# Halving sums of weight blocks in pieces of 1024 columns: a decoder trunk on one Trainium2 core

## The chip, the cores and the metric

One core of a Trainium2 chip runs the whole program in one launch. The metric is device time in microseconds. PE is TensorE, DVE is VectorE, ACT is ScalarE, POOL is GpSimd, SP issues the loads.

## The reference

A decoder trunk of two layers over x of 512 tokens x 1024 features, in fp32. Each layer adds half a SwiGLU, then a mixer, then another half SwiGLU; a norm ends the trunk. So there are four SwiGLUs (called ffn 0 to 3 here), with the even mixer between ffn 0 and 1 and the odd one between ffn 2 and 3, and nothing between ffn 1 and 2:

```python
for l in range(DEPTH):                      # DEPTH = 2
    h = _rmsnorm(x, ffn_pre_norm[l])
    x = x + 0.5 * _swiglu(h, ffn_pre_w_gate[l], ffn_pre_w_up[l], ffn_pre_w_down[l])
    h = _rmsnorm(x, mix_norm[l])
    if l % 2 == 0:
        x = x + _retention_dilated_mixer(h, ab_w_in[l // 2], ab_w_out[l // 2])
    else:
        x = x + _gla_mixer(h, gla_w_in[l // 2], gla_w_a2[l // 2], gla_b_a[l // 2], gla_w_out[l // 2])
    h = _rmsnorm(x, ffn_post_norm[l])
    x = x + 0.5 * _swiglu(h, ffn_post_w_gate[l], ffn_post_w_up[l], ffn_post_w_down[l])

def _swiglu(h, wg, wu, wd):                 # hidden width 2816
    return (jax.nn.silu(h @ wg) * (h @ wu)) @ wd
```

## The kernel before, in words

Every fp32 matrix is split in two halves, a high one (a copy in the format fp32r, on ACT) and a low one (the rest, a subtraction on DVE), and every product is three matmuls: high x high, high x low, low x high (`mm3`, L205 to L207). x stays in SBUF as eight tiles of 128 features x 512 tokens.

An ffn has 22 tiles of 128 hidden features. The first four (HEAD = 2 pairs) are projected tile by tile (`proj_t`), while `moving` (L370) builds from x and the norm's row r the activations for the rest: for each of four k a tile hh (high, L387 and L392 on ACT) and hl (low, L393 and L394 on DVE), each with seven slots of 256 columns. The row r comes from sums of squares (POOL, L270), matmuls over ones (L280) and two diagonals (DVE, L296) that PE spreads over the partitions (L298); both diagonals use one buffer.

The other 18 tiles go in nine pairs, one `block` for gate and one for up, 18 blocks in an ffn and 72 in all. A block multiplies a 2 x 2 arrangement of weight quarters (A11, A12, A21, A22, 512 columns each) with a 2 x 2 arrangement of activations by the scheme of Strassen and Winograd: seven products (P0 to P6 here, in the order in which `block` calls `product`) of 12 matmuls of 256 columns in place of eight. It needs sums of weights, S1 to S4: S1 = A21 + A22, S2 = S1 less A11, S3 = A11 less A21, S4 = A12 less S2 (signs are put into the stored weights, so that each is an add). After two of its products a block calls `fill`, which runs a down-projection tile of an earlier group (12 matmuls of 512 columns in most groups). `save` copies partial results out of the accumulator (L414, ACT) before the next product overwrites it.

The weights come by a plan, a list of steps that `weights` works off ahead of their use as far as `room` lets it (three pieces ahead for whole tiles, AHEAD = 4 for sums). A block's steps are the nested functions of `block_plan` (L117): `c0` loads 1 MB as raw (L139, issued by SP; two buffers), halves the first two quarters as one piece of 1024 columns (L142, L147) and begins the sums; `s1`, `s2`, `s3`, `a22`, `s4` each halve one piece of 512 columns: `high` is the copy (L125, tile shi), `low` the subtraction (L131, tile slo), `add` the sums (L135). shi and slo have six buffers of 512 columns each (SUMS = 6). `run` puts a chunk of down weights (L106, L107: tiles whi, wlo) into the plan after four steps of a block.

The program is written in this order, and a scheduler then sets the order of each engine from it; an engine takes its instructions strictly in that order. A tile's buffer is reused when its last reader is done.

```python
return [("w", c0), ("s", s1), ("s", s2), ("s", s3), ("s", a22), ("s", s4)]
```

## Time and profile before

| what | value |
|---|---|
| time, median of 3 runs (range) | 1923.32 us (1918.73 to 1923.42) |
| the profiled execution, its own time | 1920.47 us |
| its span | 1918.7 us |
| PE busy | 1889.4 us |
| DVE busy | 1383.0 us |
| ACT busy | 850.2 us |
| POOL busy | 90.1 us |

The span runs from the first to the last instruction that the profiler saw; the execution's own time has 1.8 us around it. Times in a timeline are us from the start of the span. Matmuls overlap, so their pace is read from the starts of neighbours, not from the duration of one; DVE and ACT pieces overlap a little too.

In the timeline ffn 0 has its blocks from about 68 to 365 us, ffn 1 from 700 to 972, ffn 2 from 1042 to 1339 and ffn 3 from 1605 to 1897. The even mixer lies between 365 and 650, the odd one between 1339 and 1560. The heads of the four ffns are the stretches just ahead of their blocks; ffn 2 starts at about 995, when ffn 1's last down tiles end.

### The profile page before, as it was taken

What the parts mean: (1) busy time and instruction counts of PE and PEld (TensorE: products, weight loads), DVE (VectorE), ACT (ScalarE), POOL (GpSimd) and SP (SyncE); (2) the same over time, 40 slices, a digit from 0 to 9 for tenths busy, and PEclk for the clock granted to TensorE, in tenths of its full rate; (3) what the DMA queues carried; (4) which work ended last, traced back from release to release, by engine and by line L of the source; (5) the groups of instructions that cost most, each with busy time, mean ns of one, the idle gap of its engine ahead of it and who ended that gap; (6) DMA issues with size and microseconds to landing.
All of it is one profiled execution on the core that took longest, in us unless ns stands there. A gap on an engine that the chain in (4) does not pass through costs nothing.

```text
span 1918.7 us, 28135 instructions
## 1 busy us (share of the span) xinstructions
PE 1889.4 (98%) x11360; PEld 1660.4 (87%) x11360; DVE 1383.0 (72%) x2114; ACT 850.2 (44%) x1377; POOL 90.1 (5%) x69
## 2 busy tenths in 40 slices
PE   8999999999999999999999999999999999999996
PEld 6899999877777889999988999998788888999995
DVE  7987786744555897777679878776466579777864
ACT  5544444433332554444445444444434245544441
POOL 1000000200000200000020000002000020000001
PEclk9999999999999999999999999999999999999998
DMA  5222222321111423332132322222222142323211
GB/s 199 99 104 106 100 100 78 123 77 66 50 66 39 165 88 112 109 104 105 67 124 92 110 103 100 99 89 85 88 77 67 56 156 89 118 100 110 100 67 44
DMA packets 43061, 183.81 MB, mean 96 GB/s; under 512 B 4897, under 2 KB 7201, under 8 KB 33714
## 3 DMA queue, kind: packets, MB, share of 16 engines
q1 hardware_dynamic: 39888, 177.75, 26.6%
q10 hardware_dynamic: 3042, 4.26, 0.7%
q8 instruction: 89, 1.46, 0.3%
q14 instruction: 42, 0.34, 0.1%
HBM read 179.89 MB, written 2.10 MB: 95 GB/s over the span
## 4 chain that ended last, share of the span: by engine, by line
PE 95%; DVE 3%; issue 1%; ACT 0%; POOL 0%; DMA 0%; POOLq 0%; DVEq 0%; SPq 0%; ACTq 0%
PE pj L205 17%; PE pj L206 17%; PE pj L207 17%; PE pj L404 12%; PE pj L406 12%; PE pj L405 12%; PE sc L740 1%; PE o L768 1%; PE sc L280 1%; PE sc L298 0%; PE sc L815 0%; PE tp L756 0%; DVE xgl L253 0%; DVE wlo L107 0%; PE o L972 0%
## 5 line engine op out<-in xcount | busy, mean ns | idle before, releaser
L205 PE MATMUL pj<-xgh,whi 128*128 128x512 f32 x1260 | 506.2, 402 | 8.0 <-ACT whi L106 7.1
L206 PE MATMUL pj<-xgl,whi 128*128 128x512 f32 x1260 | 493.2, 391 | 1.1 <-DVE xgl L253 1.0
L207 PE MATMUL pj<-xgh,wlo 128*128 128x512 f32 x1260 | 492.6, 391 | 0.0
L405 PE MATMUL pj<-hl,shi 128*128 128x256 f32 x1440 | 404.9, 281 | 1.5 <-DVE hl L394 1.5
L404 PE MATMUL pj<-hh,shi 128*128 128x256 f32 x1440 | 405.0, 281 | 0.8 <-ACT hh L392 0.8
L406 PE MATMUL pj<-hh,slo 128*128 128x256 f32 x1440 | 404.7, 281 | 0.0
L106 ACT CAST whi<-wraw 128x1024 fp32r<-128x1024 f32 x189 | 197.8, 1047 | 254.2 <-PE pj L206 164.1
L125 ACT CAST shi<-raw 128x512 fp32r<-128x512 f32 x288 | 178.5, 620 | 288.1 <-PE pj L405 232.6
L205 PEld LDWEIGHTS pj<-xgh,whi 128*128 128x128 f32 x1260 | 238.2, 189 | 62.0 <-issue 12.1
L107 DVE TENSOR_TENSOR wlo<-wraw,whi 128x1024 fp32r<-128x1024 f32 x189 | 236.1, 1250 | 65.5 <-ACT whi L106 64.9
L207 PEld LDWEIGHTS pj<-xgh,wlo 128*128 128x128 f32 x1260 | 237.9, 189 | 50.3 <-DVE wlo L107 0.8
L406 PEld LDWEIGHTS pj<-hh,slo 128*128 128x128 f32 x1440 | 276.6, 192 | 0.1
L206 PEld LDWEIGHTS pj<-xgl,whi 128*128 128x128 f32 x1260 | 238.2, 189 | 43.2 <-DVE xgl L253 2.2
L405 PEld LDWEIGHTS pj<-hl,shi 128*128 128x128 f32 x1440 | 270.5, 188 | 4.6 <-DVE hl L394 1.7
L404 PEld LDWEIGHTS pj<-hh,shi 128*128 128x128 f32 x1440 | 270.5, 188 | 4.0 <-ACT hh L392 1.1
L131 DVE TENSOR_TENSOR slo<-raw,shi 128x512 fp32r<-128x512 f32 x288 | 197.1, 687 | 83.4 <-ACT shi L125 83.3
L405 PE MATMUL pj<-hl,whi 128*128 128x256 f32 x576 | 162.3, 282 | 0.5 <-DVE hl L393 0.5
L404 PE MATMUL pj<-hh,whi 128*128 128x256 f32 x576 | 162.3, 282 | 0.1
L406 PE MATMUL pj<-hh,wlo 128*128 128x256 f32 x576 | 162.0, 281 | 0.0
L135 DVE TENSOR_TENSOR raw<-raw 128x512 f32<-128x512 f32 x216 | 148.5, 688 | 3.0
L519 DVE SCALAR_TENSOR_TENSOR x<-pj,x 128x512 f32<-128x512 f32 x160 | 109.6, 685 | 50.7 <-PE pj L207 50.7
L270 POOL TENSOR_TENSOR sqa<-sqa,sq 128x512 f32<-128x512 f32 x41 | 64.0, 1561 | 1061.8 <-issue 645.2
(201 smaller groups left out, 2375.0 us busy)
## 6 DMA issues: line engine op xcount, KB each, us to landing
raw<-in_w_blk SPq DMA_DIRECT2D x72, 1024.0 KB, 4.8
wraw<-in_w_down SPq DMA_DIRECT2D x88, 512.0 KB, 3.2
wraw<-in_w_gu SPq DMA_DIRECT2D x32, 512.0 KB, 3.2
wraw<-in_w_dqk SPq DMA_DIRECT2D x8, 512.0 KB, 3.4
wraw<-in_w_rqk SPq DMA_DIRECT2D x8, 512.0 KB, 3.3
...
```

What stands on the lines that cost most here:

```text
L106: self.halved = nc.scalar.copy(out=hi[:, :cols], in_=raw[:, :cols]).ins
L107: nc.vector.tensor_tensor(out=lo[:, :cols], in0=raw[:, :cols], in1=hi[:, :cols].bitcast(F32), op=ALU.subtract)
L125: nc.scalar.copy(out=hi, in_=x)
L131: nc.vector.tensor_tensor(out=lo, in0=x, in1=hi.bitcast(F32), op=ALU.subtract)
L135: nc.vector.tensor_tensor(out=out, in0=a, in1=b, op=ALU.add)
L205: mm(out, lhsT=w[0], rhs=x[0], start=first, stop=False)
L206: mm(out, lhsT=w[0], rhs=x[1], start=False, stop=False)
L207: self.last = mm(out, lhsT=w[1], rhs=x[0], start=False, stop=last).ins
L404: mm(out, lhsT=w[0][:, s], rhs=hi, start=first and k == 0, stop=False, skip_group_check=True)
L405: mm(out, lhsT=w[0][:, s], rhs=lo, start=False, stop=False, skip_group_check=True)
L406: self.last = mm(out, lhsT=w[1][:, s], rhs=hi, start=False, stop=k == KD // 2 - 1, skip_group_check=True).ins
L519: nc.vector.scalar_tensor_tensor(out=self.x[d], in0=ps, scalar=0.5, in1=self.x[d], op0=ALU.mult, op1=ALU.add)
```

## The change

The quarters of a block are stored in the order A21, A22, A11, A12 instead of A11, A12, A21, A22 (the rows of numbers are the same, `blocks` on the host only swaps halves). So:

- S1 and S3 are neighbours: one add of 1024 columns, with A21 read twice by a broadcast, writes both into a tile s13 (one buffer).
- S2 is written over A21, so that S2 and A22 are neighbours in raw and are halved as one piece. S4 is written over A12.
- s13 and s2 are halved in pieces of 1024 columns in wide buffers, two for high and two for low halves. S4 stays a piece of 512 columns (thi, tlo, two buffers). c0 halves A11 and A12, the second half of raw, as before in 1024 columns.
- A block so has two wide halvings and one narrow in place of five narrow ones, and one wide add and two narrow in place of four narrow ones. `block` keeps s13 for its products P1 and P4, and s2 for P2 and P5.
- `room` lets fewer than two wide sums and fewer than two narrow ones be ahead, and the chunk of down weights comes after three steps of the plan.

```diff
--- before.py
+++ after.py
@@ -27,7 +27,7 @@
 EPS = 1e-6
 WC = 1024
 LOOK = 3
-AHEAD, SUMS = 4, 6
+SPACE = 16
 HELD = 4
 PASS3 = 0.65
 H = T // 2
@@ -91,7 +91,7 @@
 
     def room(self, kind):
         n = sum(k == kind for k, _ in self.ready)
-        return n <= LOOK if kind == "w" else n < AHEAD and len(self.ready) < AHEAD + 2
+        return n <= LOOK if kind == "w" else n < 2
 
     def load_w(self, src, cols):
         nc = self.nc
@@ -117,17 +117,16 @@
         st = {}
         q = [slice(i * T, (i + 1) * T) for i in range(4)]
 
-        def high(key, x):
+        def wide(x):
             if not self.spaced:
                 self.spaced = True
-                self.t2k(self.fpool, "space", bufs=1, shape=[P, 16])
-            hi = self.t2k(self.fpool, "shi", F32R, SUMS, shape=[P, T])
+                self.t2k(self.fpool, "space", bufs=1, shape=[P, SPACE])
+            hi = self.t2k(self.fpool, "shi", F32R, 2, shape=[P, WC])
+            lo = self.t2k(self.fpool, "slo", F32R, 2, shape=[P, WC])
             nc.scalar.copy(out=hi, in_=x)
-            st[key] = (hi, x)
-
-        def low(key):
-            hi, x = st[key]
-            lo = self.t2k(self.fpool, "slo", F32R, SUMS, shape=[P, T])
+            return hi, lo, x
+
+        def low(hi, lo, x):
             nc.vector.tensor_tensor(out=lo, in0=x, in1=hi.bitcast(F32), op=ALU.subtract)
             return hi, lo
 
@@ -139,37 +138,31 @@
             nc.sync.dma_start(out=raw, in_=src)
             hi = self.t2k(self.wpool, "whi", F32R, shape=[P, WC])
             lo = self.t2k(self.wpool, "wlo", F32R, shape=[P, WC])
-            nc.scalar.copy(out=hi, in_=raw[:, :WC])
-            st["s3"] = self.t2k(self.fpool, "s3", bufs=1)
-            add(st["s3"], raw[:, q[0]], raw[:, q[2]])
-            add(raw[:, q[2]], raw[:, q[2]], raw[:, q[3]])
-            high("s1", raw[:, q[2]])
-            nc.vector.tensor_tensor(out=lo, in0=raw[:, :WC], in1=hi.bitcast(F32), op=ALU.subtract)
-            add(raw[:, q[0]], raw[:, q[0]], raw[:, q[2]])
-            return hi, lo
-
-        def s1():
-            high("s2", st["raw"][:, q[0]])
-            return low("s1")
+            nc.scalar.copy(out=hi, in_=raw[:, WC:])
+            s = self.t2k(self.fpool, "s13", shape=[P, WC], bufs=1)
+            two = lambda x: x.rearrange("p (a t) -> p a t", t=T)
+            add(two(s), two(raw[:, T:3 * T]), raw[:, q[0]].unsqueeze(1).broadcast_to([P, 2, T]))
+            st["s13"] = wide(s)
+            add(raw[:, q[0]], s[:, :T], raw[:, q[2]])
+            return low(hi, lo, raw[:, WC:])
+
+        def s13():
+            st["s2"] = wide(st["raw"][:, :WC])
+            return low(*st["s13"])
 
         def s2():
             raw = st["raw"]
-            high("s3", st["s3"])
-            add(raw[:, q[1]], raw[:, q[1]], raw[:, q[0]])
-            return low("s2")
-
-        def s3():
-            high("a22", st["raw"][:, q[3]])
-            return low("s3")
-
-        def a22():
-            high("s4", st["raw"][:, q[1]])
-            return low("a22")
+            add(raw[:, q[3]], raw[:, q[3]], raw[:, q[0]])
+            return low(*st["s2"])
 
         def s4():
-            return low("s4")
-
-        return [("w", c0), ("s", s1), ("s", s2), ("s", s3), ("s", a22), ("s", s4)]
+            x = st["raw"][:, q[3]]
+            hi = self.t2k(self.fpool, "thi", F32R, 2)
+            lo = self.t2k(self.fpool, "tlo", F32R, 2)
+            nc.scalar.copy(out=hi, in_=x)
+            return low(hi, lo, x)
+
+        return [("w", c0), ("v", s13), ("v", s2), ("s", s4)]
 
     def hook(self):
 
@@ -415,15 +408,17 @@
         c0 = self.weights()
         self.product(a[:, :H], c0, 0, 0, True)
         save(0)
-        self.product(b[:, H:], self.weights(), 0, 3, True)
-        self.product(a[:, :H], self.weights(), 0, 5, False)
+        s13 = self.weights()
+        self.product(b[:, H:], s13, 0, 3, True)
+        s2 = self.weights()
+        self.product(a[:, :H], s2, 0, 5, False)
         save(1)
         self.product(b[:, :H], c0, T, 1, False)
-        self.product(a[:, :H], self.weights(), 0, 4, False)
+        self.product(a[:, :H], s13, T, 4, False)
         save(2)
         nc.vector.tensor_tensor(out=part[:, 2 * H:], in0=b[:, H:], in1=part[:, 2 * H:], op=ALU.add)
         fill()
-        self.product(a[:, :H], self.weights(), 0, 6, False)
+        self.product(a[:, :H], s2, T, 6, False)
         self.product(b[:, H:], self.weights(), 0, 2, False)
         nc.vector.tensor_tensor(out=part[:, :T], in0=b, in1=part[:, :T], op=ALU.add)
         fill()
@@ -987,7 +982,7 @@
             for g, group in enumerate(BLOCKS):
                 for b in range(2 * len(group)):
                     steps = self.block_plan(a["w_blk"][f, group[b // 2] - HEAD, b % 2])
-                    self.plan += steps[:4] + [chunks[g].pop(0)] + steps[4:]
+                    self.plan += steps[:3] + [chunks[g].pop(0)] + steps[3:]
             self.plan += chunks[-1]
 
         ffn(0)
@@ -1076,7 +1071,7 @@
     def blocks(w):
 
         t = tiles(w)[2 * HEAD:]
-        return np.concatenate([t[0::2], t[1::2]], axis=2)
+        return np.concatenate([t[1::2], t[0::2]], axis=2)
 
     out["w_blk"] = np.stack([np.stack([blocks(g), blocks(u)], axis=1) for g, u, _ in ffns])
     for c, group in enumerate(GROUPS):
```

The matmuls and the loads are as many and as large as before. The scheduler sets a new order around the changed pieces. Three places are shown; the numbers behind names tell tiles apart, and lines of the changed kernel are five or seven lower than before from there on (L289 is L296, L387 is L394, L434 is L439).

**DVE at the start of ffn 0**, from the third k of `moving` to the first part of the fourth. The names: hl is a low half of activations, sg a step on the way to one, slo, tlo and wlo are low halves of weights, part is a gate or up tile times r, s_103 is the second block's s13. Before:

```order
L131 TENSOR_TENSOR slo_469<-s_78_394,shi_406 128x512
L391 SCALAR_TENSOR_TENSOR sg_442<-sg_442,sg_441 128x256
L107 TENSOR_TENSOR wlo_474<-wraw_471,whi_473 128x1024
L383 SCALAR_TENSOR_TENSOR sg_454<-x_85,gain,rrow_324 128x2x256
L394 TENSOR_TENSOR hl_446<-sg_442,hh_445 128x1024
L383 SCALAR_TENSOR_TENSOR sg_454<-x_89,gain,rrow_324 128x512
L453 TENSOR_TENSOR part_528<-pj_411,rrow_324 128x512
L388 TENSOR_TENSOR sg_455<-sg_454 128x512
L393 TENSOR_TENSOR hl_459<-sg_454,hh_458 128x768
```

Changed:

```order
L130 TENSOR_TENSOR tlo_471<-raw_389,thi_470 128x512
L384 SCALAR_TENSOR_TENSOR sg_439<-sg_439,sg_438 128x256
L134 TENSOR_TENSOR s_103_504<-raw_499 128x1024
L376 SCALAR_TENSOR_TENSOR sg_451<-x_85,gain,rrow_324 128x2x256
L387 TENSOR_TENSOR hl_443<-sg_439,hh_442 128x1024
L376 SCALAR_TENSOR_TENSOR sg_451<-x_89,gain,rrow_324 128x512
L134 TENSOR_TENSOR raw_499<-s_103_504,raw_499 128x512
L381 TENSOR_TENSOR sg_452<-sg_451 128x512
L386 TENSOR_TENSOR hl_456<-sg_451,hh_455 128x768
L383 SCALAR_TENSOR_TENSOR sg_452<-sg_452,sg_451 128x256
L130 TENSOR_TENSOR wlo_502<-raw_499,whi_501 128x1024
```

The low half of S3 and a tile times r are gone from this place, the second block's joined sum, its S2 and its c0 low half have come in, and the low half of S4 stands here.

**DVE at the start of ffn 1**, around the two diagonals (diag) that spread r. Before:

```order
L283 TENSOR_SCALAR var_5796<-sc_5791 128x4
L292 CAST colh_5831<-rcol_5790 128x4
L293 TENSOR_TENSOR colh_5831<-rcol_5790,colh_5831 128x4
L296 TENSOR_TENSOR diag_5834<-ident,colh_5831 128x512
L107 TENSOR_TENSOR wlo_5802<-wraw_5799,whi_5801 128x1024
L131 TENSOR_TENSOR slo_5982<-raw_5967,shi_5976 128x512
L296 TENSOR_TENSOR diag_5837<-ident,colh_5831 128x512
L107 TENSOR_TENSOR wlo_5845<-wraw_5842,whi_5844 128x1024
```

Changed:

```order
L276 TENSOR_SCALAR var_5634<-sc_5629 128x4
L285 CAST colh_5669<-rcol_5628 128x4
L107 TENSOR_TENSOR wlo_5640<-wraw_5637,whi_5639 128x1024
L286 TENSOR_TENSOR colh_5669<-rcol_5628,colh_5669 128x4
L289 TENSOR_TENSOR diag_5672<-ident,colh_5669 128x512
L130 TENSOR_TENSOR slo_5814<-s_1037_5810,shi_5813 128x1024
L130 TENSOR_TENSOR slo_5819<-raw_5805,shi_5818 128x1024
L134 TENSOR_TENSOR s_1062_5920<-raw_5915 128x1024
L289 TENSOR_TENSOR diag_5675<-ident,colh_5669 128x512
L107 TENSOR_TENSOR wlo_5683<-wraw_5680,whi_5682 128x1024
```

The first block's two wide low halves and the second block's joined sum now stand between the diagonals, and a low half of head weights ahead of the first. The start of ffn 3 reads alike in both.

**DVE at the end of ffn 1**, where the last tiles of x are written and x becomes the input of ffn 2 (xgl). Before:

```order
L547 SCALAR_TENSOR_TENSOR x_86<-pj_9189,x_86 128x512
L131 TENSOR_TENSOR slo_9510<-raw_9495,shi_9504 128x512
L253 SCALAR_TENSOR_TENSOR xgl_9204<-x_86,gain,xgh_9203 128x512
L547 SCALAR_TENSOR_TENSOR x_87<-pj_9210,x_87 128x512
L107 TENSOR_TENSOR wlo_9230<-wraw_9227,whi_9229 128x1024
L547 SCALAR_TENSOR_TENSOR x_88<-pj_9233,x_88 128x512
L253 SCALAR_TENSOR_TENSOR xgl_9268<-x_87,gain,xgh_9267 128x512
L253 SCALAR_TENSOR_TENSOR xgl_9272<-x_88,gain,xgh_9271 128x512
L547 SCALAR_TENSOR_TENSOR x_89<-pj_9250,x_89 128x512
L107 TENSOR_TENSOR wlo_9290<-wraw_9287,whi_9289 128x1024
L253 SCALAR_TENSOR_TENSOR xgl_9276<-x_89,gain,xgh_9275 128x512
```

Changed:

```order
L542 SCALAR_TENSOR_TENSOR x_86<-pj_8865,x_86 128x512
L542 SCALAR_TENSOR_TENSOR x_87<-pj_8886,x_87 128x512
L107 TENSOR_TENSOR wlo_8906<-wraw_8903,whi_8905 128x1024
L246 SCALAR_TENSOR_TENSOR xgl_8880<-x_86,gain,xgh_8879 128x512
L130 TENSOR_TENSOR slo_9185<-raw_9171,shi_9184 128x1024
L542 SCALAR_TENSOR_TENSOR x_88<-pj_8909,x_88 128x512
L246 SCALAR_TENSOR_TENSOR xgl_8944<-x_87,gain,xgh_8943 128x512
L134 TENSOR_TENSOR s_1552_9286<-raw_9281 128x1024
L542 SCALAR_TENSOR_TENSOR x_89<-pj_8926,x_89 128x512
L246 SCALAR_TENSOR_TENSOR xgl_8948<-x_88,gain,xgh_8947 128x512
L107 TENSOR_TENSOR wlo_8966<-wraw_8963,whi_8965 128x1024
L246 SCALAR_TENSOR_TENSOR xgl_8952<-x_89,gain,xgh_8951 128x512
```

The low half of the first block's S2 and A22 and the second block's joined sum now stand among the last four tiles, in place of the narrow low half of S1.

On ACT, in the steady run of blocks, the order ahead of the third save of a block is: the high half of the next block's s13, then the save, then the high half of its s2 (before: narrow high halves at these places). In the first block of ffn 0 the high half of the third block's c0 now stands ahead of the second save.

## Rows read from the trace of the kernel before

**Rows 1.** Page, part 1: busy us (share of the span) and instructions, by engine.

```profile
PE 1889.4 (98%) x11360; PEld 1660.4 (87%) x11360; DVE 1383.0 (72%) x2114; ACT 850.2 (44%) x1377; POOL 90.1 (5%) x69
```

**Rows 2.** Busy us by stretch: length, engines, granted PE clock, DMA share, GB/s.

```profile
57.00:68.00 11.00, 7.26 (x22) 4.92 (x22) 11.00 (x17) 4.57 (x7) 0.00 (x0) 0.69 0.15 48
68.00:365.00 297.00, 297.00 (x2026) 276.06 (x2025) 230.75 (x338) 141.83 (x241) 10.39 (x7) 1.00 0.31 107
...
972.00:1000.00 28.00, 26.90 (x115) 21.71 (x114) 23.92 (x28) 15.08 (x22) 11.66 (x8) 0.94 0.31 111
```

**Rows 3.** What PE waited for, whole program: total us, times, longest.

```profile
PE pj L405 <- DVE hl L394: 1.5, 1, 1.5
...
PE pj L206 <- DVE xgl L253: 1.0, 1, 1.0
```

**Rows 4.** Groups by line and form: busy us, mean ns | idle before, what ended it.

```profile
L131 DVE TENSOR_TENSOR slo<-raw,shi 128x512 fp32r<-128x512 f32 x288 | 197.1, 687 | 83.4 <-ACT shi L125 83.3
L125 ACT CAST shi<-raw 128x512 fp32r<-128x512 f32 x288 | 178.5, 620 | 288.1 <-PE pj L405 232.6 <-DVE slo L131 22.0 <-DVE raw L135 16.0
...
L135 DVE TENSOR_TENSOR raw<-raw 128x512 f32<-128x512 f32 x216 | 148.5, 688 | 3.0
...
L147 DVE TENSOR_TENSOR wlo<-raw,whi 128x1024 fp32r<-128x1024 f32 x72 | 87.7, 1218 | 0.2 <-ACT whi L142 0.2
...
L142 ACT CAST whi<-raw 128x1024 fp32r<-128x1024 f32 x72 | 75.5, 1049 | 36.3 <-PE pj L405 27.9 <-PE pj L206 6.1 <-DMA raw<-in_w_blk 1.2
```

**Rows 5.** Timeline of ACT in a block: start us, us, line, idle before.

```profile
805.01 0.62 ACT L125 CAST shi<-raw 128x512 fp32r<-128x512 f32 x1 [0.36 <-PE pj L405]
805.54 0.37 ACT L414 COPY part<-pj 128x256 f32<-128x256 f32 x1
```

**Rows 6.** Timeline of PE in the same block.

```profile
804.93 0.39 PE L205 MATMUL pj<-xgh,whi 128*128 128x512 f32 x1
...
807.65 0.28 PE L404 MATMUL pj<-hh,shi 128*128 128x256 f32 x1
```

**Rows 7.** Page, part 6: the blocks' loads, KB each, median us to landing.

```profile
raw<-in_w_blk SPq DMA_DIRECT2D x72, 1024.0 KB, 4.8
```

**Rows 8.** Timeline of DVE, start of ffn 0.

```profile
65.14 1.22 DVE L394 TENSOR_TENSOR hl<-sg,hh 128x1024 fp32r<-128x1024 f32 x1
66.27 0.68 DVE L454 TENSOR_TENSOR sg<-part,sg 128x512 f32<-128x512 f32 x1
66.88 0.68 DVE L451 TENSOR_TENSOR sg<-pj,rrow 128x512 f32<-128x512 f32 x1
```

**Rows 9.** Timeline of PE, start of ffn 0.

```profile
60.07 0.38 PE L405 MATMUL pj<-hl,shi 128*128 128x256 f32 x1 [1.47 <-DVE hl L394]
...
67.61 0.41 PE L405 MATMUL pj<-hl,shi 128*128 128x256 f32 x1
```

**Rows 10.** Timeline of DVE, start of ffn 1.

```profile
655.15 0.68 DVE L131 TENSOR_TENSOR slo<-raw,shi 128x512 fp32r<-128x512 f32 x1
657.67 0.69 DVE L296 TENSOR_TENSOR diag<-ident,colh 128x512 fp32r<-128x512 f32 x1 [1.83 <-PE sc L298]
```

**Rows 11.** Timeline of PE, start of ffn 1.

```profile
658.42 0.50 PE L298 MATMUL sc<-diag,ones_r 128*128 128x512 f32 x1
```

**Rows 12.** Timeline of DVE, end of ffn 1.

```profile
980.04 3.48 DVE L253 SCALAR_TENSOR_TENSOR xgl<-x,gain,xgh 128x512 fp32r<-128x512 f32 x2
...
984.90 0.75 DVE L253 SCALAR_TENSOR_TENSOR xgl<-x,gain,xgh 128x512 fp32r<-128x512 f32 x1 [0.19 <-ACT xgh L252]
...
989.89 1.45 DVE L253 SCALAR_TENSOR_TENSOR xgl<-x,gain,xgh 128x512 fp32r<-128x512 f32 x1 [0.27 <-ACT xgh L252]
...
993.31 1.44 DVE L253 SCALAR_TENSOR_TENSOR xgl<-x,gain,xgh 128x512 fp32r<-128x512 f32 x1 [0.24 <-ACT xgh L252]
```

**Rows 13.** Timeline of POOL, end of ffn 1.

```profile
979.76 3.20 POOL L270 TENSOR_TENSOR sqa<-sqa,sq 128x512 f32<-128x512 f32 x2 [1.93 <-ACT sq L266]
```

**Rows 14.** Timeline of PE, end of ffn 1.

```profile
995.38 0.95 PE L280 MATMUL sc<-ones,sqa 128*128 128x1 f32 x8
```

## The prediction, made before the changed kernel was run

> **What bounds the kernel now.** I read the page's list of engines first: PE is busy for 1889.4 of 1918.7 us, DVE for 1383.0, ACT for 850.2 [rows 1]. The change issues the same matmuls on the same numbers of columns, and it edits work of ACT and DVE alone, so it can move the time only where PE stands still or will stand still. The busy times by stretch show where that is [rows 2]. In 68 to 365 us, the blocks of the first ffn, PE has 297.00 busy of 297.00 us while DVE has 230.75. In 57 to 68 it is the reverse: DVE has 11.00 of 11.00, PE 7.26, at a granted clock of 0.69 on the mean, so partly at 1.2 instead of 2.4 GHz. In 972 to 1000, where ffn 1 ends and ffn 2 begins, PE lacks 1.1 us and the clock is 0.94. The list of what PE waited for over the whole program has rows for halved activations (hl, L394, 1.5 us) and for the next stage's input (xgl, L253, 1.0) [rows 3]; no row of that list names a weight piece (shi, slo). So nothing in the 72 blocks can be gained, and what can be gained or lost lies at the edges of the four ffns.
>
> **Work removed.** By the groups of the edited lines [rows 4] a halved pair of 512 columns takes 620 ns on ACT and 687 on DVE for each piece, one of 1024 takes 1049 and 1218. Per block ACT issues two wide copies for four narrow ones, 2 x (2 x 620 - 1049) = 382 ns less. DVE saves 2 x (2 x 687 - 1218) = 312 ns on the halves and, a 512 add taking 688, about 158 ns on the joined add: 0.47 us by summed durations. By starts it is less: a 1024 piece follows its predecessor by 1.13 us, a 512 piece by 0.61 or 0.60 [rows 8], so three joinings save about 0.08 us each, 0.24 us. Over 72 blocks that is 27 us of ACT and 17 to 34 us of DVE. I cost it at nothing: both engines have spare time in the blocks, PE has none.
>
> **The steady block.** What could fail is the cover, since each wide piece holds one of two buffers instead of one of six. The order has the next block's s13 halving directly ahead of the third save of part on ACT, and it waits there for P4, the last reader of its buffer. Before, a 512 halving stood there: it began at 805.01, the save at 805.54 [rows 5]; P4 had ended by 804.93, when the down-projection began, and P5, which overwrites what is saved, began at 807.65 [rows 6]. With 1049 ns for 620 the save ends at about 805.01 + 1.05 + 0.37 = 806.4, and 1.2 us remain. The s2 halving waits for P5 in the same way, with a whole down tile and three more products until it is wanted. The last reader of raw is now s2's low half (before, s4's); the next 1 MB load lands in 4.8 us [rows 7], less than the two down tiles of a block take by themselves, 2 x 2.72 [rows 6]. Sum for the 72 blocks: 0.
>
> **The start of ffn 0.** Here DVE sets PE's pace. Up to the last hl (L394 of the fourth k, 65.14 us) [rows 8] the new order has two joined adds for one 512 add, two wide low halves and one narrow for three narrow, one more 1024 low half of a weight (the second block's c0), and two 512 steps moved behind: +2.26 - 0.60 + 2.26 + 0.60 - 1.80 + 1.13 - 1.20 = +2.65 us of DVE. Of that, 0.93 comes ahead of the second k, where DVE still has gaps; I count half of it as absorbed, which leaves 2.2. PE waited 1.47 us for hl at 60.07 and used the fourth one at 67.61 [rows 9], 1.3 us after it was written, with other matmuls between; the new order fills this place with P0 of the second block instead, which leaves about as much to do behind. I take +2.2 us. Bounds: 0, if PE's other work covers it all, and +5, if the clock takes another 1.7 us, as it does at the end of ffn 1 (0.06 of 28 us [rows 2]), and one ACT wait of 1.1 us is added (the third block's c0 halving, 1049 ns, now stands ahead of the first block's second save and waits for P3).
>
> **The starts of ffn 1 and ffn 3.** The row of r is spread by two diagonals in one buffer. Between them DVE had one weight and one 512 low half, then 1.83 us of waiting for PE [rows 10]. Now the weight goes ahead of the first diagonal (1.13), and two wide low halves and the second block's joined add stand between: 3 x 1.13 = 3.39 against 1.13 + 0.60 + 1.83 = 3.56 but all of it 1.13 later, so the second diagonal comes about 0.9 us later. PE took it at 658.42, just after it was done (657.67 + 0.69) [rows 10, 11], so nothing covers the delay: +0.9 us at each of the two starts, where the order reads alike. Bounds 0 and 1.6 each.
>
> **The end of ffn 1.** DVE adds each x and writes its xgl, PE waits for the last. From x of the seventh tile on, the new order has a wide low half and the next block's joined add (2.26) where a 512 low half stood (0.60): +1.66. DVE's waits for ACT there, 0.19 + 0.27 + 0.24 [rows 12], take up about 0.5. So +1.2 us; bounds -0.5 and +3.3 (all the wide pieces of that stretch, nothing taken up).
> One row there speaks of a second price. Two xgl took 3.48 us together, one alone 0.75 [rows 12], while POOL had its adds of squares running, two in 3.20 [rows 13]. The Trainium skill (SBUF — State Buffer, on the port pair that DVE and GpSimd share) says that a DVE operation with two SBUF inputs and a GpSimd operation exclude each other for a whole instruction. The row agrees that they stretch each other; it does not show a full block. By the page a wide DVE piece would hold off POOL for up to its whole length, and the sum would be the third rival's; by the row I leave it out, since PE needs POOL's sum only at 995.38 [rows 14].
>
> **Sum.** 0 + 2.2 + 2 x 0.9 + 1.2 = +5.2 us. The mixers, the start of ffn 2 and the tail have the same pieces in the same places: 0. The profiled execution took 1920.5 us (1.8 outside its span), so **1925.7 us**. That execution lies 2.8 below the median of the three runs and inside their spread. A measurement here tells 0.3%, 5.8 us, from no change, so my sum is just short of it.
>
> **Rivals.**
> 1. A wait in every block: the wide halving ahead of the third save starts later than P4's end by more than the 1.2 us left (it also waits for s13's add), and PE stands before P5. It decides from 1.2 us on; at 0.2 us a block it costs 14 us beside the edges: 1940. Against it: DVE has 22% idle in the blocks [rows 2], and the add is done a block ahead. For it: two buffers where six were.
> 2. Faster: of the 11.0 us at the start of ffn 0 at most 22 x 0.227 = 5.0 are matmuls (2.72 us for twelve of the longer kind [rows 6]), so 6 are lost, and the end of ffn 1 loses 1.1 of gap and 1.7 of clock. If the smaller DVE work per block let the starts run ahead, as joined pieces save 0.08 us each and PE's clock recovered earlier, half of these 8.8 could come back: 1916. Against it: the order puts more DVE work ahead of hl there, not less.
> 3. POOL and DVE hold each other up: three ffn starts take their squares from POOL beside the new wide pieces. At one wide piece each, 1.13 us, that is 3.4 on the sum: 1929.
> 4. Nothing happens, because PE's other matmuls cover every delay: 1920.5.
> 5. ffn 0's start goes to its bound of +5, clock and ACT wait both: 1928.5 or, with the boundary's +3.3 too, 1930.6.
>
> **How the numbers follow.** My sum 0.48, rival 1 0.14, rival 2 0.09, rival 3 0.07, rival 4 0.12, rival 5 0.10. The edges' bounds add up to -0.5 and +11.5 (5 + 3.2 + 3.3); with the runs' spread of 2 below and 3 above the profiled one the range is 1918 to 1936. It leaves out most of rivals 1 and 2. Faster by over 0.3%: 0.07, from rival 2. Slower: rivals 1, 3 and 5 at 0.31, and 0.11 of my own sum's upper side, 0.42. Within: 0.51. The likeliest case by itself spans 1922 to 1930.
>
> **What would show it.** Right: PE still without a wait on shi or slo in the blocks; the groups at 1.05 and 1.22 us; the last hl of ffn 0 near 67.3 instead of 65.14; a wait of PE's second spreading matmul for its diagonal of about 0.9 us, twice; a last xgl that starts near 994.5 instead of 993.31. Wrong: PE gaps before P5 in every block (rival 1), a start of ffn 0 that ends before 68 us (rival 2), longer POOL adds with a wait at L280 (rival 3), or a saving in a stretch where PE is full now, which no view of this trace would explain.

## The result, and the profile after

The changed kernel takes 1934.52 us in the median of 5 runs (1928.88 to 1934.99), the kernel before 1918.73 in the 5 runs beside it (1917.44 to 1923.42). The ratio estimated from all these runs is 1.007, 95% interval 1.0058 to 1.0081 (that of the two medians alone is 1.008). It is slower, by more than 0.3%. The profiled execution has a span of 1933.2 us, 14.5 more than the one that the prediction worked from.

The page's first part, and the busy times by stretch (columns as in [rows 2]) of the changed kernel:

```profile
PE 1896.5 (98%) x11360; PEld 1664.3 (86%) x11360; DVE 1343.7 (70%) x1898; ACT 823.1 (43%) x1233; POOL 91.5 (5%) x69
```

```profile
57.00:68.00 11.00, 4.38 (x15) 2.58 (x14) 11.00 (x18) 3.09 (x5) 0.00 (x0) 0.71 0.43 144
68.00:365.00 297.00, 297.00 (x2021) 276.30 (x2021) 217.84 (x284) 135.24 (x208) 8.88 (x6) 0.99 0.30 103
...
700.00:972.00 272.00, 271.98 (x1910) 254.95 (x1909) 196.34 (x257) 119.83 (x186) 0.00 (x0) 1.00 0.29 101
...
1000.00:1042.00 42.00, 39.81 (x161) 32.28 (x162) 34.16 (x48) 15.98 (x20) 2.72 (x3) 0.88 0.27 89
...
1339.00:1560.00 221.00, 219.53 (x1050) 180.31 (x1049) 131.44 (x216) 85.88 (x109) 19.16 (x16) 0.98 0.22 74
...
1605.00:1897.00 292.00, 291.98 (x2015) 272.15 (x2014) 213.16 (x282) 129.30 (x197) 0.00 (x0) 1.00 0.27 94
```

ACT is busy 27 us less than in [rows 1], as forecast, DVE 39 us less, a little more than the 17 to 34, and it bought nothing: in the blocks PE is as full as before ([rows 2]; 272 us in 700 to 972 have 271.98). The new gaps are mainly at 57 to 68 and in 1000 to 1042, and the clock is lower, 0.99, 0.88 and 0.98, in three stretches that had 1.00 before. (The stretches are cut at the same times in both kernels, so work that is late in the changed one falls into a later stretch.) The list of what PE waited for, whole program, answers to [rows 3]:

```profile
PE sc L291 <- DVE diag L289: 7.4, 8, 1.9
...
PE pj L199 <- DVE xgl L246: 3.5, 3, 1.6
...
PE pj L397 <- ACT hh L385: 1.8, 1, 1.8
...
PE pj L398 <- DVE hl L387: 1.5, 1, 1.5
```

Before, diagonals cost 5.5 us and xgl 1.0. The groups of the edited lines (columns as in [rows 4]) are of the sizes that the pieces of 1024 columns had before:

```profile
L130 DVE TENSOR_TENSOR slo<-s,shi 128x1024 fp32r<-128x1024 f32 x72 | 89.3, 1241 | 18.2 <-ACT shi L126 18.2
...
L134 DVE TENSOR_TENSOR s<-raw 128x1024 f32<-128x1024 f32 x72 | 88.1, 1223 | 3.3 <-DMA raw<-in_w_blk 3.3
...
L126 ACT CAST shi<-s 128x1024 fp32r<-128x1024 f32 x72 | 75.7, 1051 | 39.1 <-PE pj L398 32.0 <-DVE s L134 5.7 <-PE pj L399 1.4
```

**Where the 14.5 us are.** Both kernels issue the same number of matmuls, so the n-th one of one trace can be set against the n-th of the other. The table gives, for each stretch between two such matmuls, how many us it became longer than in the first profile of the kernel before (numbers of the matmuls: 200, 1000, 2000, 3600, 4000, 5600, 6400, 8000, 9000, 9600, 11300). The second column is a second profile of the changed kernel, the third one of the kernel before; E1 to E10 are the experiments below.

| stretch | after | after, again | before, again | E1 | E2 | E3 | E4 | E5 | E6 | E7 | E8 | E9 | E10 |
|---|---|---|---|---|---|---|---|---|---|---|---|---|---|
| head of ffn 0 | 0.4 | -0.4 | -1.1 | -0.1 | -0.7 | -0.9 | 0 | 0.3 | -0.9 | -0.2 | -1.6 | -0.6 | -0.3 |
| start of ffn 0 | 3.1 | 2.9 | 1.0 | -0.9 | 4.5 | 4.6 | -0.5 | 3.8 | 2.2 | 3.2 | 0.6 | -1.0 | -0.2 |
| its blocks | 0 | 0 | 0 | 0.9 | 0 | 0 | 0 | 0 | 0 | 0 | 0 | 0 | 0 |
| its end, even mixer | 0 | 0 | 0 | 3.9 | 0 | 0 | -0.6 | 0.2 | 2.2 | -0.2 | -0.2 | -0.7 | 0 |
| start of ffn 1 | 1.9 | 3.9 | 0 | 4.4 | 0.6 | 0.7 | 1.0 | 1.1 | 0.2 | 1.1 | 0 | 0.9 | 0.1 |
| its blocks | 0 | 0 | 0 | 1.1 | -0.1 | 0 | 0 | 0 | 0 | 0 | 0 | 0 | 0 |
| end of ffn 1, start of ffn 2 | 5.0 | 5.6 | -1.6 | 4.6 | 4.6 | 0.6 | 5.8 | -1.9 | 1.0 | -3.2 | -3.3 | -2.1 | -3.0 |
| blocks of ffn 2 | 0 | 0 | 0 | 1.2 | 0 | 0 | 0 | 0 | 0 | 0 | 0 | 0 | 0 |
| odd mixer | 3.3 | 3.1 | 0.1 | 1.6 | 0 | 0.1 | -0.1 | 3.4 | 3.8 | -0.2 | 1.4 | -0.1 | 0 |
| start of ffn 3 | 0.7 | 0.8 | -0.1 | 0.9 | -0.2 | 0.6 | 0.2 | 1.2 | 0.1 | 0.7 | -0.1 | 0.8 | 0 |
| its blocks | 0 | 0 | 0 | 1.3 | 0 | 0 | 0 | 0 | 0 | 0 | 0 | 0 | 0 |
| sum | 14.5 | 15.8 | -1.7 | 19.0 | 8.7 | 5.7 | 5.7 | 8.1 | 8.5 | 1.1 | -3.1 | -2.7 | -3.5 |

So nothing is lost in the 72 blocks. But for the 0.4 us of the head of ffn 0, which the second profile has the other way, all is lost at five places: the starts of ffn 0, 1 and 3, the end of ffn 1 and the odd mixer.

**Start of ffn 0.** The DVE timeline of the changed kernel has the second block's joined add, S2 and c0 low half ahead of the last hl:

```profile
59.07 1.22 DVE L134 TENSOR_TENSOR s<-raw 128x1024 f32<-128x1024 f32 x1
...
62.67 0.69 DVE L134 TENSOR_TENSOR raw<-s,raw 128x512 f32<-128x512 f32 x1
...
65.08 1.22 DVE L130 TENSOR_TENSOR wlo<-raw,whi 128x1024 fp32r<-128x1024 f32 x1
...
67.75 1.22 DVE L387 TENSOR_TENSOR hl<-sg,hh 128x1024 fp32r<-128x1024 f32 x1
```

That hl starts at 67.75 instead of 65.14 [rows 8], with 0.4 of it from the head. PE's half clock (1.2 GHz) lasted 10.2 us here, against 6.8 in the first profile of the kernel before. The second profile of the kernel before had 10.2 too, and lost 1.0 at this edge with nearly the same waits: with the half clock alike, the change loses 2.1 here.

**Start of ffn 1.** DVE, around the diagonals, and PE's second spreading matmul:

```profile
654.66 1.23 DVE L134 TENSOR_TENSOR s<-raw 128x1024 f32<-128x1024 f32 x1 [2.79 <-DMA raw<-in_w_blk]
...
656.53 0.15 DVE L276 TENSOR_SCALAR var<-sc 128x4 f32<-128x4 f32 x1
...
659.71 1.22 DVE L130 TENSOR_TENSOR slo<-s,shi 128x1024 fp32r<-128x1024 f32 x1
660.85 1.22 DVE L130 TENSOR_TENSOR slo<-raw,shi 128x1024 fp32r<-128x1024 f32 x1
661.98 1.22 DVE L134 TENSOR_TENSOR s<-raw 128x1024 f32<-128x1024 f32 x1
663.12 0.68 DVE L289 TENSOR_TENSOR diag<-ident,colh 128x512 fp32r<-128x512 f32 x1
```

```profile
663.86 0.50 PE L291 MATMUL sc<-diag,ones_r 128*128 128x512 f32 x1 [1.50 <-DVE diag L289]
```

Three wide pieces stand between the diagonals, and the second one is at 663.12: before it was at 657.67 [rows 10], which with the 3.56 us already lost is 661.23. PE waits 1.50 us for it. The first row shows what was not foreseen: the first block's joined add stands ahead of the steps to r and waits 2.79 us for its load, with DVE behind it. In the kernel before an add of 512 columns stood there and waited 2.10 (its DVE timeline):

```profile
650.40 0.69 DVE L135 TENSOR_TENSOR s<-raw 128x512 f32<-128x512 f32 x1 [2.10 <-DMA raw<-in_w_blk]
...
651.84 0.16 DVE L283 TENSOR_SCALAR var<-sc 128x4 f32<-128x4 f32 x1
```

With 0.7 more of waiting and 0.5 more of adding, the variance, the first step to r, comes 1.1 us later (656.53, against 651.84 and the 3.56). From the variance to the second diagonal it is 6.59 us instead of 5.83, another 0.8.

**End of ffn 1.** DVE and POOL in the changed kernel:

```profile
985.40 2.31 DVE L130 TENSOR_TENSOR slo<-s,shi 128x1024 fp32r<-128x1024 f32 x1
...
994.51 2.31 DVE L130 TENSOR_TENSOR slo<-raw,shi 128x1024 fp32r<-128x1024 f32 x1
...
998.00 1.21 DVE L134 TENSOR_TENSOR s<-raw 128x1024 f32<-128x1024 f32 x1
...
1000.82 2.30 DVE L107 TENSOR_TENSOR wlo<-wraw,whi 128x1024 fp32r<-128x1024 f32 x1
1003.04 0.74 DVE L246 SCALAR_TENSOR_TENSOR xgl<-x,gain,xgh 128x512 fp32r<-128x512 f32 x1
```

```profile
983.32 5.55 POOL L263 TENSOR_TENSOR sqa<-sqa,sq 128x512 f32<-128x512 f32 x3 [325.54 <-issue]
992.57 3.17 POOL L263 TENSOR_TENSOR sqa<-sqa,sq 128x512 f32<-128x512 f32 x2 [3.71 <-ACT sq L259]
998.29 2.06 POOL L263 TENSOR_TENSOR sqa<-sqa,sq 128x512 f32<-128x512 f32 x1 [2.55 <-ACT sq L259]
1000.68 1.36 POOL L263 TENSOR_TENSOR sqa<-sqa,sq 128x512 f32<-128x512 f32 x1 [0.33 <-ACT sq L259]
```

Three pieces of 1024 columns, two of them the change's and one a low half of a weight, took 2.31, 2.31 and 2.30 us instead of 1.22, each beside an add of POOL, and the last xgl started at 1003.04. In the kernel before it started at 993.31 [rows 12], 9.7 us earlier; 5.5 of these had been lost by then. It matters which of the two begins first: the joined add at 998.00 took its usual time, and the add that POOL began 0.29 us after it took 2.06 us instead of the last one's 1.36.

The wait for xgl is only about half of the 5.0 us. It grew from 1.0 us in all to 3.5; the rest is the clock. TensorE ran at 1.2 GHz for 10.2 us around this edge, against 3.4 in the first profile of the kernel before; PE stood still for about 2 us of the 10.2, so the longer half clock cost about 2.4 us by this estimate. Busy times of the same stretch (columns as in [rows 2]) before, in the changed kernel, and in E7 below, which has neither the waits nor the half clock:

```profile
975.00:1015.00 40.00, 38.90 (x167) 31.38 (x166) 32.27 (x41) 19.33 (x29) 11.66 (x8) 0.96 0.28 97
```

```profile
975.00:1015.00 40.00, 36.55 (x145) 28.81 (x143) 29.63 (x33) 17.49 (x24) 12.91 (x8) 0.87 0.30 105
```

```profile
975.00:1015.00 40.00, 40.00 (x181) 33.00 (x180) 33.40 (x47) 22.38 (x31) 1.01 (x1) 1.00 0.34 120
```

**Odd mixer.** No wait of PE grew here. The loss is the clock's: 6.8 us at half clock, with PE busy throughout, is 3.4 us of its work. In the stretch with the low-rank projection (matmuls of 17 rows) the clock was granted in full before, and not after (rows of before, then of the changed kernel):

```profile
1345.00:1365.00 20.00, 20.00 (x80) 14.47 (x79) 6.57 (x9) 13.46 (x14) 0.00 (x0) 1.00 0.23 79
```

```profile
1355.00:1375.00 20.00, 20.00 (x66) 13.41 (x65) 5.04 (x6) 12.45 (x13) 0.00 (x0) 0.83 0.25 80
```

### The profile page after: what moved, and what is told of

Its sections match the earlier page's. It is cut to its first block, busy times and chain, and to the rows that moved or that the text cites. A ratio compares the mean times of both kernels' runs of the same rounds, so it can differ in the third digit from the quotient of the medians.

```text
span 1933.2 us, 27572 instructions
## 1 busy us (share of the span) xinstructions
PE 1896.5 (98%) x11360; PEld 1664.3 (86%) x11360; DVE 1343.7 (70%) x1898; ACT 823.1 (43%) x1233; POOL 91.5 (5%) x69
## 5 line engine op out<-in xcount | busy, mean ns | idle before, releaser
L397 PE MATMUL pj<-hh,shi 128*128 128x256 f32 x1152 | 324.2, 281 | 1.9 <-ACT hh L385 1.8
L398 PE MATMUL pj<-hl,shi 128*128 128x256 f32 x1152 | 324.1, 281 | 1.5 <-DVE hl L387 1.5
L399 PE MATMUL pj<-hh,slo 128*128 128x256 f32 x1152 | 323.9, 281 | 0.0
L130 DVE TENSOR_TENSOR wlo<-raw,whi 128x1024 fp32r<-128x1024 f32 x72 | 88.3, 1226 | 218.3 <-ACT whi L141 218.2
L397 PEld LDWEIGHTS pj<-hh,shi 128*128 128x128 f32 x1152 | 216.4, 188 | 5.9 <-ACT hh L385 2.2
L399 PEld LDWEIGHTS pj<-hh,slo 128*128 128x128 f32 x1152 | 221.3, 192 | 0.0
L398 PEld LDWEIGHTS pj<-hl,shi 128*128 128x128 f32 x1152 | 216.5, 188 | 4.5 <-DVE hl L387 1.7
L407 ACT COPY part<-pj 128x256 f32<-128x256 f32 x216 | 79.6, 369 | 159.5 <-PE pj L399 159.4
L126 ACT CAST shi<-raw 128x1024 fp32r<-128x1024 f32 x72 | 75.4, 1048 | 125.3 <-PE pj L398 119.1
```

What stands on the lines that cost most here:

```text
L126: nc.scalar.copy(out=hi, in_=x)
L130: nc.vector.tensor_tensor(out=lo, in0=x, in1=hi.bitcast(F32), op=ALU.subtract)
L397: mm(out, lhsT=w[0][:, s], rhs=hi, start=first and k == 0, stop=False, skip_group_check=True)
L398: mm(out, lhsT=w[0][:, s], rhs=lo, start=False, stop=False, skip_group_check=True)
L399: self.last = mm(out, lhsT=w[1][:, s], rhs=hi, start=False, stop=k == KD // 2 - 1, skip_group_check=True).ins
L407: save = lambda i: nc.scalar.copy(out=part[:, i * H:(i + 1) * H], in_=a[:, :H])
```

## The experiments

Theory A: weight work that the plan brings forward is queued on DVE ahead of what PE waits for at the edges. Theory B: the wide pieces themselves, wherever they stand. Theory C: the half clock by chance. Theory D: DVE and POOL hold each other up, and a piece of 1024 columns that meets an add of squares takes twice its time. All differences below are of the table.

**E1. S4 later, so that the second block's c0 comes later.**

```diff
-        return n <= LOOK if kind == "w" else n < 2
+        v = sum(k == "v" for k, _ in self.ready)
+        return n <= LOOK if kind == "w" else n < 2 if kind == "v" else n < 1 and v < 2
```

> The changed kernel, with room stricter: the narrow sum S4 is only prepared once the block has taken s13, so the second block's c0 and its sums no longer come ahead of the first block. At the start of ffn 0 the last low half of activations then stands about 2.9 us of DVE work earlier; at the starts of ffn 1, 2 and 3 the order of DVE is that of the changed kernel. Theory A (the time is lost at the edges, at ffn 0 by weight work brought forward): the start of ffn 0 loses no more than in the kernel before, 3.1 us less than in the changed kernel, everything else stays; span about 1930, 1928 to 1931. Theory B (the width of the pieces by itself makes DVE late at the edges, whatever is brought forward): within 1 us of the changed kernel's 1933.2. Rival of the clock alone (the half clock falls by chance, the edges' waits do not matter): the shift behind ffn 0 stays 3.5 us or changes without its waits changing.

Measured: 1937.85 us, ratio to before 1.0095 (1.008 to 1.011), slower than the change. The start of ffn 0 came back as theory A has it, -0.9 instead of 3.1. But the expectation of the whole failed: new losses of 3.9 us at the end of ffn 0 and about 1 us in each ffn's blocks appeared. From PE's waits of this run:

```profile
PE pj L199 <- DVE x L543: 2.1, 1, 2.1
...
PE pj L398 <- ACT part L408: 0.3, 2, 0.2
```

PE waited for an accumulator that an x step of DVE frees, and in two blocks for a save on ACT; the saves are 0.3 us of the 4.5 that the four rows of blocks lost. Why the accumulators fall so in this version, and where the rest of the 4.5 went, was not followed.

**E2. Wide buffers, narrow instructions.** `low2` is the same loop around `low`.

```diff
-            nc.scalar.copy(out=hi, in_=x)
+            for i in range(2):
+                nc.scalar.copy(out=hi[:, q[i]], in_=x[:, q[i]])
...
-            add(two(s), two(raw[:, T:3 * T]), raw[:, q[0]].unsqueeze(1).broadcast_to([P, 2, T]))
+            for i in range(2):
+                add(s[:, q[i]], raw[:, q[i + 1]], raw[:, q[0]])
...
-            return low(*st["s13"])
+            return low2(*st["s13"])
```

> The changed kernel with each piece of s13 and s2 halved, and S1 and S3 added, in two instructions of 512 columns; layout, buffers, plan and look-ahead stay those of the change. Theory A: the same weight work stands at the edges, so the span stays within 3 us of the changed kernel's 1933.2, with the start of ffn 0 late by 3 us as there. Theory B: with narrow pieces the edges go back, the shift behind ffn 0 under 1 us, that behind the end of ffn 1 under 2, span 1919 to 1925. Both: no wait of PE in the blocks, DVE 20 us busier.

Measured: 1931.28 us, ratio 1.0062 (1.0045 to 1.0079). The start of ffn 0 stays at 4.5 and the end of ffn 1 at 4.6: width is not what makes these two late, against theory B. The start of ffn 1 falls to 0.6, where the low halves of S1 and S3 go, as narrow pieces, ahead of the first diagonal (657.01 and 658.82, the diagonal at 659.50); at this edge width does count. At the end of ffn 1 POOL's adds stretch other pieces in turn (DVE timeline of this run; 0.68 and 1.22 are the usual times):

```profile
984.24 1.79 DVE L131 TENSOR_TENSOR slo<-s,shi 128x512 fp32r<-128x512 f32 x1
985.95 2.31 DVE L107 TENSOR_TENSOR wlo<-wraw,whi 128x1024 fp32r<-128x1024 f32 x1
...
999.95 1.75 DVE L140 TENSOR_TENSOR s<-raw 128x512 f32<-128x512 f32 x1
```

**E3. The kernel before with more look-ahead.**

```diff
-AHEAD, SUMS = 4, 6
+AHEAD, SUMS = 6, 6
```

> The kernel before, with AHEAD = 6 in place of 4: all five narrow pieces of a block and then the second block's c0 and sums are prepared ahead. Its order of DVE brings the second block's sums and c0 ahead of the last low half of activations at the start of ffn 0, as in the changed kernel, and leaves the starts of ffn 1 and 3 as they were. Theory A: the start of ffn 0 is 2 to 4 us later than in the kernel before, the rest the same; 1921 to 1924 against a span of 1918.7. Theory B: no change, within 1 us.

Measured: 1925.81 us, ratio 1.0032 (1.002 to 1.0044). The start of ffn 0 loses 4.6 with narrow pieces; sums and c0 of the second block stand before the last hl here too (DVE timeline):

```profile
60.88 0.68 DVE L135 TENSOR_TENSOR s<-raw 128x512 f32<-128x512 f32 x1
...
64.22 1.22 DVE L147 TENSOR_TENSOR wlo<-raw,whi 128x1024 fp32r<-128x1024 f32 x1
...
65.96 1.22 DVE L394 TENSOR_TENSOR hl<-sg,hh 128x1024 fp32r<-128x1024 f32 x1
```

Here and in E2 the half clock lasted 13.7 us, which is why 4.6 come out where the last hl is only 1.7 us late (0.8 by [rows 8], 0.9 from an earlier head). The expected 2 to 4 us were a little short, and 0.6 us each at three later edges came on top. So the cause at the start of ffn 0 is settled: it is the look-ahead that came with the new plan, theory A. How long the half clock lasts there is not (6.8, 10.2 or 13.7 us in these runs).

**E4. As E1, and a buffer for each diagonal** (one instead of two for S4's halves).

```diff
-            diag = self.t2k(self.misc, "diag", F32R, bufs=1)
+            diag = self.t2k(self.misc, "diag", F32R, bufs=2)
...
-            hi = self.t2k(self.fpool, "thi", F32R, 2)
-            lo = self.t2k(self.fpool, "tlo", F32R, 2)
+            hi = self.t2k(self.fpool, "thi", F32R, 1)
+            lo = self.t2k(self.fpool, "tlo", F32R, 1)
```

> As the first run, and the two diagonals that spread r get a buffer each, which puts them next to each other on DVE (room for it: one buffer instead of two for the halves of S4). Theory A: PE's waits for the second diagonal at the starts of ffn 1 and 3, 1.7 and 0.6 us, are gone too; 2.6 us less than the first run by the shifts there, span about 1927.5. Theory B: the pieces are still wide, 1932 to 1934. A wait for S4's halves inside the blocks would show as more than 5 us over the first run, and in PE's waits by the names thi and tlo.

Measured: 1924.74 us, ratio 1.0026 (1.0016 to 1.0036), better than expected, since E1's new losses are not there. The low halves now come behind both diagonals:

```profile
654.45 0.69 DVE L290 TENSOR_TENSOR diag<-ident,colh 128x512 fp32r<-128x512 f32 x1
655.05 1.22 DVE L131 TENSOR_TENSOR slo<-s,shi 128x1024 fp32r<-128x1024 f32 x1
```

The starts of ffn 1 and 3 lose 1.0 and 0.2. The end of ffn 1 keeps its 5.8.

**E5. c0's work on DVE queued behind the second diagonal** while an ffn's first tiles are projected (`self.edge` is that diagonal's instruction, `hold` is set around the loop of these tiles):

```diff
-            add(two(s), two(raw[:, T:3 * T]), raw[:, q[0]].unsqueeze(1).broadcast_to([P, 2, T]))
...
+            with self.tc.issue_after(self.edge) if self.hold else nullcontext():
+                add(two(s), two(raw[:, T:3 * T]), raw[:, q[0]].unsqueeze(1).broadcast_to([P, 2, T]))
...
```

> The changed kernel, with one rule added for DVE's order: what c0 issues on DVE while an ffn's first four tiles are projected is queued behind the second diagonal of that ffn. Pieces, buffers, plan and look-ahead are those of the change. On DVE no weight sum then stands among the xgl of the end of ffn 1 or between the diagonals of ffn 1 and 3; the start of ffn 0 is nearly as in the changed kernel. Theory A (weight work queued ahead of what PE waits for at the edges): behind the start of ffn 1 the shift against the kernel before grows by under 0.7 us instead of 1.9, behind the end of ffn 1 by under 1.5 instead of 5.0, behind the start of ffn 3 by nothing; ffn 0 keeps its 3.5. Span 1922 to 1926. Theory C (the waits there come from the wide pieces and the clock, wherever the pieces stand): the shift still grows by 3 us or more at the end of ffn 1, span above 1928.

Measured: 1926.52 us, ratio 1.0033 (1.002 to 1.0045). The end of ffn 1 goes from 5.0 to -1.9, with pieces as wide as in the change; the start of ffn 1 keeps 1.1 and that of ffn 3 1.2, more than expected. At both, PE now waits 0.6 us for a gate or up tile on DVE (part, L449). At the end of ffn 1 it is place, not width.

**E6. As E5, and a later c0 behind the last hl.**

```diff
-            with self.tc.issue_after(self.edge) if self.hold else nullcontext():
+            with self.tc.issue_after(self.edge_h if len(self.hs) == KD // 2 else self.edge) if self.hold else nullcontext():
...
```

> As the run before, and c0 of a block that is prepared after the last low half of activations has been written down in the program is queued behind that low half on DVE. This moves the second block's sums and c0 behind it at the start of ffn 0 too, with the look-ahead of the change and wide pieces. Theory A: the start of ffn 0 comes back to the kernel before or earlier (shift -1 to +1 instead of 3.5); with the other edges as in the run before, the span is 1917 to 1922, and the median within 3 us of the kernel before. Theory B: 1928 or more. If a wait of PE appears at the second block, the queue was made too strict: then the shift grows between the first and the third block of an ffn.

Measured: 1929.59 us, ratio 1.0049 (1.0035 to 1.0063): a miss. The start of ffn 0 improved less than hoped, 2.2 instead of 3.8, and waits for x as in E1 came back, about 2.2 us each at the ends of ffn 0, 1 and 2. The third one (at 1341.34) falls into the stretch of the odd mixer and is 2.2 of its 3.8; the rest goes with 3.4 us of half clock.

**E7 and E8. No adds of squares on POOL,** in the changed kernel and in the kernel before.

```diff
-        nc.gpsimd.tensor_tensor(out=self.sqacc, in0=self.sqacc, in1=sq, op=ALU.add)
```

Each norm's sum then leaves out seven of the eight tiles of x.

> The changed kernel without POOL's adds of squares (seven of eight tiles of x are left out of each norm's sum). The order of DVE at the end of ffn 1 is row by row that of the changed kernel. Theory D (DVE and POOL hold each other up, and a wide piece that meets an add of squares takes twice its time): the wide pieces there take 1.22 us instead of 2.31, and the shift at the end of ffn 1 against the next kernel is 2.5 us or less instead of 5.0. Theory A alone (the number of pieces in the queue): it stays at 4 or more.

> The kernel before, also without POOL's adds of squares, to compare the run before with. Theory D: the xgl at the end of ffn 1 take 0.75 us each instead of up to 1.74, and PE's wait for the last of them, 1.0 us, is gone or halved. Otherwise: 1.0 us as before.

Measured: one run each, 1920.27 and 1916.44 us. The DVE timeline of E7 has the two wide low halves, the weight's and the last xgl of the end of ffn 1, and E8 has two xgl together, 3.48 in [rows 12], and the last one:

```profile
983.28 1.22 DVE L130 TENSOR_TENSOR slo<-s,shi 128x1024 fp32r<-128x1024 f32 x1
...
989.53 1.22 DVE L130 TENSOR_TENSOR slo<-raw,shi 128x1024 fp32r<-128x1024 f32 x1
...
994.32 1.22 DVE L107 TENSOR_TENSOR wlo<-wraw,whi 128x1024 fp32r<-128x1024 f32 x1
995.45 0.75 DVE L246 SCALAR_TENSOR_TENSOR xgl<-x,gain,xgh 128x512 fp32r<-128x512 f32 x1
```

```profile
978.48 1.41 DVE L253 SCALAR_TENSOR_TENSOR xgl<-x,gain,xgh 128x512 fp32r<-128x512 f32 x2
...
989.90 0.75 DVE L253 SCALAR_TENSOR_TENSOR xgl<-x,gain,xgh 128x512 fp32r<-128x512 f32 x1 [0.24 <-ACT xgh L252]
```

All three pieces take 1.22 us again. From the first x to the last xgl DVE needs 25.4 us in the changed kernel (977.65 to 1003.04) and 19.5 in E7 (975.99 to 995.45); in the kernel before 21.1 (972.17 to 993.31), in E8 18.9 (971.00 to 989.90). So POOL costs DVE 5.9 us with the new pieces there and 2.2 without, and the longer queue by itself 0.6. The edge is at -3.2 in E7 and at -3.3 in E8: without POOL's adds PE has no wait and the full clock there in both, and the change loses nothing at the end of ffn 1. Theory D, and theory A only in that the pieces stand where POOL works.

The runs bear on the start of ffn 1 too. In E7 and E8 the first block's add waits equally long for its load (1.93 and 1.91 us), and the edge loses 1.1 instead of 1.9: with the longer wait gone, about what the pieces between the diagonals cost by themselves is left. Why the load keeps it waiting longer in the changed kernel was not followed.

The Trainium skill (SBUF — State Buffer, section "SBUF: two separate sides", on the port pair that DVE and GpSimd share) has an exclusive lock for a whole instruction. These two runs agree with it: a wide piece of 1.22 us grows by 1.09, which is about one add of POOL (1.36 us for the last one in the rows of the changed kernel, and POOL's spans are rough). So does the joined add at 998.00, which kept its time while the add of POOL behind it grew.

**E9. E4 and E5 together.**

```diff
-        return n <= LOOK if kind == "w" else n < 2
...
+        return n <= LOOK if kind == "w" else n < 2 if kind == "v" else n < 1 and v < 2
...
+            with self.tc.issue_after(self.edge) if self.hold else nullcontext():
...
+            diag = self.t2k(self.misc, "diag", F32R, bufs=2)
...
```

> The changed kernel with the three edits of the fourth and fifth run together: S4 prepared after s13 is taken, a buffer for each diagonal and one for S4's halves, and c0 of the first blocks queued behind the second diagonal on DVE. Theory A with D: the start of ffn 0 as in the fourth run (shift about -0.5), the starts of ffn 1 and 3 without a wait, the end of ffn 1 at -3 by itself as in the fifth run; without the half clock in the odd mixer the span is 1915 to 1917, with it 1918 to 1920. Faster than the kernel before by 0 to 3 us in the median. Theory B (wide pieces cost time of their own): 1922 or more.

Measured: 1916.32 us in 11 runs (1915.89 to 1916.94), ratio 0.9983 (0.9974 to 0.9992): faster than the kernel before (1919.46 in the 21 runs beside it), by 3 us, where the change has 1.007. By stretch (columns as in [rows 2]):

```profile
975.00:1000.00 25.00, 25.00 (x115) 20.55 (x114) 19.75 (x25) 12.58 (x18) 11.97 (x8) 1.00 0.33 105
1345.00:1370.00 25.00, 25.00 (x96) 18.67 (x95) 8.36 (x11) 13.00 (x13) 0.00 (x0) 0.93 0.23 75
```

In 975 to 1000 PE has no gap and the full clock. The odd mixer's 0.93 cost nothing in the end (-0.1).

**E10. The kernel before with E5's rule.**

```diff
-            add(st["s3"], raw[:, q[0]], raw[:, q[2]])
...
+            with self.tc.issue_after(self.edge) if self.hold else nullcontext():
+                add(st["s3"], raw[:, q[0]], raw[:, q[2]])
...
```

> The kernel before with the queueing rule of the fifth run alone: c0 of the first blocks behind the second diagonal. Narrow pieces, AHEAD as it was. Theory A with D: the end of ffn 1 falls by 3 us against the kernel before, as in the fifth run, as no weight sum is left there to meet POOL's adds; the other edges stay within 1; span 1915 to 1917. Then the run before it gains nothing by its wide pieces. If the end of ffn 1 stays as it was, the gain of the fifth run came from something that the wide pieces need.

Measured: 1920.89 us in 11 runs (1916.54 to 1922.29), ratio 1.0003 (0.9994 to 1.0012). The profile shows the -3.0 that was expected at the end of ffn 1, the runs show no gain: the profiled execution, 1917.0 us, is one of the four of 11 below 1919. The other seven lie between 1920.8 and 1922.3, with a mean granted clock of 0.991 where the four have 0.993 or 0.994; where they lose it was not profiled. The kernel before with all of E9's edits was not run, so that the wide pieces gain time of their own is not shown.

**E11 and E12. The changed kernel and the kernel before once more, without an edit.**

> The changed kernel once more, for one more profile of it. Waits that come from the order (theory A, D) repeat: shifts of 3.5 behind the start of ffn 0, 1.9 at ffn 1, 0.7 at ffn 3, within 0.5; at the end of ffn 1 5.0 within 1. The half clock in the odd mixer, 3.2 us in the first profile, repeats if it follows from the order, and need not if it is chance; one of the five runs of this kernel, at 1928.9 against 1934.5, would be such a one.

> The kernel before once more, for one more profile of it: the same waits within 0.5 us at each edge. Its half clock at the start of ffn 0 and at the end of ffn 1 repeats if the order decides; in the odd mixer there was none.

Measured: 1936.24 and 1918.37 us, one run each. The losses that come from the order repeated at the start of ffn 0 (2.9), the end of ffn 1 (5.6) and the start of ffn 3 (0.8), with more scatter than the expected 0.5 where the head of ffn 0 is counted in; the start of ffn 1 took 3.9 instead of 1.9, with a stretch of half clock that the first profile had not.

In the kernel before the waits repeated, but the half clock did not, against what was expected if the order decides it: 10.2 us instead of 6.8 at the start of ffn 0, and none instead of 3.4 at the end of ffn 1, where the edge is at -1.6 with the same wait of 1.0 us for xgl. So 1.0 to 1.6 us of a single edge in a single profile can be the clock alone, as theory C has it.

The odd mixer lost 3.1 again, and nothing again in the kernel before. So there it is not plain chance; but E2, E3, E7, E9 and E10 lost nothing there, E5 3.4, E1 1.6, and E8, with the order of the kernel before, 1.4, and in none of these did a wait of PE there grow. What decides it stays open, and theory C with it for these 3 us.

## Why the prediction was right, and where it was not

The forecast was slower by 5.2 us within 1918 to 1936. It came out slower, inside the range, by 14.5 us between the profiles: beyond the 1922 to 1930 of the likeliest case, which also had it just short of 0.3%. That it stayed inside is partly luck: the end of ffn 1 went past its bound (5.0, bound 3.3), so did the start of ffn 1 (1.9, bound 1.6), and the odd mixer lost 3.3 where 0 was taken, while the starts of ffn 0 and 3 stayed below their bounds. By the forecast's own terms (1920.5, 11.5 and 3) the upper end is 1935, not 1936; the result lies inside either.

- **What bounds the kernel, and the blocks at 0:** right, and shown by PE's full stretches, by the zeros of the table and by its list of waits, which names no shi or slo. Rival 1 fell with them, rival 4 too.
- **Start of ffn 0, +2.2:** the mechanism was right and nearly the size, 3.1 and 2.9. The last hl came 2.6 us later, 2.2 without the head's 0.4. The rest fits the longer half clock, which stood in the bound only and which the kernel before showed in its second profile too (1.0). Of rival 5 the clock came, the wait for a save on ACT did not. E1 and E3 show the cause from both sides.
- **Starts of ffn 1 and 3, +0.9 each:** 1.9 and 3.9 at ffn 1, 0.7 and 0.8 at ffn 3. The step that failed at ffn 1 is the 0.9 that was taken for all of it, from the pieces between the variance and the second diagonal. The working did not look ahead of the variance, where a joined add that waits for its load made all of it 1.1 us later; these pieces themselves cost 0.8, and both together are the 1.9 measured.
- **End of ffn 1, +1.2:** the term that failed most, 5.0 and 5.6. The sum took the pieces at their own times and left POOL out "by the row". The row that it cited, two xgl in 3.48 us, showed how much an add of squares takes from DVE; the sum put that on POOL's account alone, asked when PE needs POOL's result, and not how long DVE's pieces become. Rival 3 had the mechanism, with one wide piece at each of three starts; at this one three pieces of 1024 columns met POOL's adds, and xgl did too. The forecast read the row as no full block; E8 has the same two xgl in 1.41 us, so two adds had cost them 2.07. It also had no term for the clock here, which is about half of the 5.0 and goes with PE's longer waits: E5, E7, E8, E9 and E10, without those waits, have the full clock at this edge. E7 and E8 show the cause.
- **The mixers at 0:** wrong for the odd one, 3.3 and 3.1, by the clock. The forecast had no term for a fall of the clock where no wait changes, and why it falls there is open.
- **Rival 2, faster:** not for the change; E9 shows that the edges held such a gain, once the work stood elsewhere.
